# Sample attention's weighted sum of values: from three elementwise engines to 32-column products on TensorE

## The chip, the core and the metric

The kernel runs on one core of a Trainium2 chip. The metric is the device time of one launch in microseconds (us). Engines are named as the profile does: PE is TensorE, PEld its weight loads, DVE VectorE, ACT ScalarE, POOL GpSimd, SP the engine that issues every DMA here.

## The reference, cut to what matters

One decoder layer is computed for 1,024 prompt tokens and for eight sample tokens. Layer: an FFN, an input projection, two mixers (a gated recurrence and a differential attention, four heads each), an output projection, a second FFN. All of it is float32.

For a sample token the attention looks at 4,096 cached positions, 32 pages of 128, in each of four heads, with two softmax maps per head:

```python
p = jax.nn.softmax(jnp.concatenate(scores, axis=-1), axis=-1)
p = p.reshape(B, DA_HEADS, 2, Lq, p.shape[-1])
a = p[:, :, 0] - lam * p[:, :, 1]
...
    outs.append(jnp.einsum('bhqk,bkhv->bqhv', a[..., start:start + n], v.astype(jnp.float32)))
```

The last line is the one that the change concerns, for the cached part: eight rows, 32 pages, a page being 128 positions by four heads of 128 values, 256 KB.

## The kernel before

**Stages.** The prompt goes through the weights in two halves of 512 tokens; the eight sample tokens ride along as columns. `first_half` is FFN1 and the input projection, `second_half` the output projection and FFN2. The program's order is first half 0, first half 1, second half 0, second half 1. Weights come as tiles of 128x512 (`wr`), are split on ACT and DVE (partly POOL) into a high and a low part (`wH`, `wL`, seven buffers each), and every product is three PE passes (`mm3`, L376; L431 for the down projection; L498 for the input projection), in slices of 512, 264 or 256 columns. There are 672 such weight tiles; second half 1 begins with the 525th.

**Work beside.** `weave` interleaves two side streams with this main work, by credits: `mixer` (the prompt's recurrence and attention, one half at a time), and `sample_stream`: `sample_attention`, then `hgrn_sample`. Second half 1 needs the result of both for its second slice (the tile `oTs`). The framework then orders each engine's instructions by a simulated time line with priorities: main evacuations first, mixers next, the sample stream last. Engines run their instructions in that order, and SP's one DMA queue too.

**Sample attention.** For sample row b, `keys(b, i)` loads a page of keys, multiplies it on POOL (L954) and sums it on DVE (L955). When 32 pages are through, `softmax(b)` makes the weights `Sb` [128 positions, 32 pages, 8 maps]; its last instruction adds the two maps of a head (map two already carries minus lambda). `values(b, i)` then goes through 32 pages of values, one by one, interleaved with the keys of row b + 1: on even pages four DVE instructions, one a head, multiply by a weight and add to `sacc` [128, 512] (L1004); on odd pages four ACT instructions scale the page (L1006) and POOL adds it (L1008); page 0 is ACT's (L1002). `end(b)` sums `sacc` over the positions by four products with a column of ones (L1015).

**Rings that matter here.** Pages of both kinds, and the recurrence's states, share the ring `kv` of eight buffers in program order. PSUM tiles: `mm` (main work) three, `mx` two (until now the mixers alone), `my` two, and `nm` one: the sums of the norms, `softmax`, `end` and the recurrence take turns in it, in program order. So `norm_factors` of first half 1 (L270, L279), which comes after `end(2)` and `softmax(3)` in the program, cannot begin before these are through, and the evacuations of the input projection (L498) need its factors.

Of the kernel before, what the change touches and what calls it, by code (L numbers as in the profile page):

```python
# [18 lines left out]
P = 128  # L19
# [9 lines left out]
# columns of the constant table  # L29
C_ID, C_M, C_SUF, C_MSK, C_REL, C_SREL, C_SLP, C_QSC = 0, 128, 1152, 1280, 1728, 2752, 2784, 2792  # L30
C_N = 2800


def shape_constants():
# [5 lines left out]
    for l in range(7):  # L40
        s = 64 >> l
        mid = (t // (2 * s)) * 2 * s + s
        right = (t >= mid) & (j >= mid) & (j <= t)
        left = (t < mid) & (j > t) & (j < mid)
        c[:, C_M + (l + 1) * P:C_M + (l + 2) * P] = right | left
        same = (j // (2 * s)) == (t // (2 * s))
        # the columns of right halves alone
        c[:, C_MSK + l * 64:C_MSK + (l + 1) * 64] = (same & (j % (2 * s) < s))[:, (np.arange(P) // s) % 2 == 1]
# [6 lines left out]
    c[:, C_QSC:C_QSC + 8] = np.repeat(SLOPES, 2)[None, :] ** 2  # L55
    return c
# [3 lines left out]
def kernel(ctx: ExitStack, tc: tile.TileContext, I, O):  # L60
# [63 lines left out]
    slp = CT("slp", [P, 8])  # L124
    c1n = CT("c1n", [P, 512])
# [9 lines left out]
    def load_consts():  # L135
        SP.dma_start(srel, K[:, C_SREL:C_SREL + NPG])
        SP.dma_start(slp, K[:, C_SLP:C_SLP + 8])
        SP.dma_start(pages, I["page_table"].rearrange("b (o n) -> o (b n)", o=1))
        # lower bound: c1n = -(1 - lb) / 2 with lb the softmax over the two rows
# [13 lines left out]
        # lambda  # L153
# [11 lines left out]
        # gains of the mixers  # L165
# [18 lines left out]
    # rows of the sample tokens  # L184
# [15 lines left out]
    class Group:  # L200
        """tokens that pass the weights together: tiles as wide as the group"""
# [9 lines left out]
    class Slice:  # L211
        """columns of a group that one matrix product takes"""
# [53 lines left out]
    def norm_sums(sl):  # L266
        """sums of squares by block, down the partitions; the columns of each height"""
# [6 lines left out]
    def norm_spread(sl, R, r):  # L274
        """the factors along a row, on all partitions"""
# [23 lines left out]
    def scaled(gi, sl, d):  # L299
        """what norm_finish makes, but for the norm's factors: those come with the products' results"""  # L300
# [6 lines left out]
    def norm_row(sl):  # L307
        """the factors alone, along a row"""
# [26 lines left out]
    def xn_pair(w):  # L335
        """room for high and low parts: in one tile, or one each"""
# [13 lines left out]
    def wload(H, L, raw, src):  # L350
        # while DVE has the most to do, some of the low parts on Pool
# [7 lines left out]
    def wtile(src, c):  # L359
        """c columns of weights, from tiles of 512 / c blocks of rows: pairs of (high, low) parts"""  # L360
# [9 lines left out]
    def mm3(ps, W, sl):  # L370
        """ps = W^T x, weights stationary, in three passes"""
# [7 lines left out]
    FB = [2, 4, 4, 4, 4, 4]  # L379

    def ffn(pre, slices, done, deferred=False):
        wg, wu, wd = (I[pre + n] for n in ("_w_gate", "_w_up", "_w_down"))

        def gateup(f, hs):
# [30 lines left out]
            # by slices where what comes before goes by slices  # L415
# [104 lines left out]
    def evac(name, c, ps, tb, kind, row, factors):  # L520
        # of the norm: the factor, half of it, and the eps that it makes of EPS and of 64 EPS
# [15 lines left out]
        else:  # L537
# [9 lines left out]
            with tc.high_priority():  # L547
                if name == "aq":
                    # the scale of the scores over each head's slope comes with the norm
# [6 lines left out]
        # where it goes  # L556
# [15 lines left out]
        else:  # L572
# [3 lines left out]
            # high and low parts side by side, and so below each other once transposed  # L576
# [43 lines left out]
    def hgrn_head(b):  # L620
        """the logarithms of the decays"""
# [8 lines left out]
    def hgrn_block(b):  # L630
# [30 lines left out]
        def stage1(h, q):  # L661
            """decays of four levels (the first of the first half: the running one), and both sides' factors"""
# [19 lines left out]
        def stage2(h, q):  # L682
# [11 lines left out]
            def right(t, l):  # L694
                """the columns of right halves at a level"""
# [72 lines left out]
    def att_scores(h, b, KT):  # L768
        """softmax weights of both maps, combined"""
        negrel = hc["negrel"]  # L770
        n = (b + 1) * P
        # both parts of the queries, each against the keys' high and low parts
# [74 lines left out]
    def zcols(n):  # L847
        """rows of the sample tokens as columns, by heads"""
# [68 lines left out]
    def page(name, src, i):  # L917
        t = kv()
        if i % 4 == 0:
            # the next numbers are read only once earlier pages are on their way: few registers  # L920
# [6 lines left out]
    def sample_attention():  # L927
# [3 lines left out]
        # scores of the new keys  # L931
# [25 lines left out]
        def softmax(b):  # L957
# [32 lines left out]
            S4 = Sb.rearrange("p i (h j) -> p i h j", j=2)  # L990
            DVE.tensor_tensor(out=S4[:, :, :, 0], in0=S4[:, :, :, 0], in1=S4[:, :, :, 1], op=ALU.add)

        def values(b, i):
            a = S[b][0]
            vt = page("v", cv, b * NPG + i)
            if i == 0:
                S["acc"] = ST("sacc", [P, 512], bufs=1)
            acc = S["acc"]
            for h in range(4):
                hs, w = slice(h * P, (h + 1) * P), a[:, i, 2 * h:2 * h + 1]  # L1000
                if i == 0:
                    ACT.activation(acc[:, hs], vt[:, hs], AF.Copy, scale=w)  # L1002
                elif i in VDVE:
                    DVE.scalar_tensor_tensor(out=acc[:, hs], in0=vt[:, hs], scalar=w, in1=acc[:, hs], op0=ALU.mult, op1=ALU.add)  # L1004
                else:
                    ACT.activation(vt[:, hs], vt[:, hs], AF.Copy, scale=w)  # L1006
            if i and i not in VDVE:
# [252 lines left out]
```

## Time and profile before

| what | value |
|---|---|
| median of three runs | 2474.95 us (2472.2 to 2476.01) |
| span of the profiled execution | 2471.9 us |
| PE busy | 2304.7 us, 93% |
| DVE busy | 1827.5 us, 74% |
| ACT busy | 1071.8 us, 43% |
| POOL busy | 999.5 us, 40% |
| chain that ended last | PE 22% of the span, every other engine at most 1% |

The profiled execution's span lies 3.1 us below the median of the runs. Matmuls are pipelined: the duration of one is its latency, and the distance from start to start is what it costs when the next one waits behind it. PEclk is the share of full TensorE clock that was granted, as a mean of its two levels (1.2 and 2.4 GHz) over a stretch. The chain followed back from the end covers about the last quarter of the span.

### The profile page before, as it was taken

Reading aid. Unit: us, or ns where it says so; the run is one execution under the profiler, and the core shown is the slowest. Engines: PE = TensorE matmul, PEld = TensorE weight load, DVE = VectorE, ACT = ScalarE, POOL = GpSimd, SP = SyncE. Lnnn points to the kernel's source line nnn. Section 1 sums busy time; section 2 is a strip of 40 time slices with the busy share of each in tenths; the row PEclk is TensorE's granted clock in tenths of the full one; section 3 lists DMA queues with packets and bytes.
Section 4 is the critical chain, followed back from the end, with each engine's and each line's share of the span. In section 5 each row is a group of like instructions: output and inputs, shape, how many; then the busy total and the mean of one; then the engine's idle time right before and its main releaser. Section 6 shows DMA issues by size and latency. Waiting matters only on the chain. (4 is left out here: it accounts for less than half of the span.)

```text
span 2471.9 us, 44310 instructions
## 1 busy us (share of the span) xinstructions
PE 2304.7 (93%) x15101; PEld 2079.1 (84%) x15101; DVE 1827.5 (74%) x3750; ACT 1071.8 (43%) x2465; POOL 999.5 (40%) x788
## 2 busy tenths in 40 slices
PE   7999999989998978989899879889798999999999
PEld 6999999989877866767888767677687889999999
DVE  6555657596799796798798997997987766555554
ACT  4322324435544434545554643434465554322222
POOL 4100101381176374474684673785756310100000
PEclk9999999999998998999899999999999999999999
DMA  4332334684466467576785773566755652332332
GB/s 137 90 95 83 112 91 125 183 286 139 130 217 205 134 213 230 165 234 215 239 280 145 243 236 114 186 211 202 235 173 182 183 170 94 90 95 91 90 95 74
DMA packets 273396, 402.37 MB, mean 163 GB/s; under 512 B 29641, under 2 KB 104650, under 8 KB 273170
## 3 DMA queue, kind: packets, MB, share of 16 engines
q1 hardware_dynamic: 273170, 399.54, 52.0%
q8 instruction: 119, 1.95, 0.3%
q14 instruction: 107, 0.88, 0.1%
HBM read 361.22 MB, written 38.21 MB: 162 GB/s over the span
## 5 line engine op out<-in xcount | busy, mean ns | idle before, releaser
L376 PE MATMUL mm<-xn,wH 128*128 128x256 f32 (+2 forms) x4800 | 1121.8, 327 | 19.4 <-DVE xn L106 5.7
L376 PEld LDWEIGHTS mm<-xn,wH 128*128 128x128 f32 x4800 | 808.6, 192 | 94.8 <-DVE xn L106 8.1
L376 PE MATMUL mm<-xn,wL 128*128 128x256 f32 (+2 forms) x2400 | 782.7, 326 | 1.4 <-DVE wL L106 1.4
L106 ACT CAST wH<-wr 128x512 fp32r<-128x512 f32 x672 | 409.3, 617 | 518.1 <-PE mm L376 275.3
L106 DVE TENSOR_TENSOR wL<-wr,wH 128x512 fp32r<-128x512 f32 x504 | 414.7, 825 | 163.8 <-ACT wH L106 132.8
L431 PE MATMUL mm<-h,wH 128*128 128x264 f32 (+2 forms) x2112 | 487.0, 324 | 7.3 <-DVE ft L409 4.7
L376 PEld LDWEIGHTS mm<-xn,wL 128*128 128x128 f32 x2400 | 461.1, 192 | 36.8 <-DVE wL L106 1.8
L954 POOL TENSOR_TENSOR kv<-kv,ss 128x512 f32<-128x512 f32 x256 | 371.2, 1459 | 145.3 <-DMA kv<-in_cache_k 127.1
L431 PEld LDWEIGHTS mm<-h,wH 128*128 128x128 f32 x2112 | 349.9, 190 | 38.4 <-DVE ft L409 5.8
L411 POOL TENSOR_TENSOR ft<-ft,acc 128x256 f32<-128x256 f32 (+1 forms) x110 | 101.5, 922 | 656.6 <-DVE ft L409 645.9
L431 PE MATMUL mm<-h,wL 128*128 128x264 f32 (+2 forms) x1056 | 340.5, 323 | 0.0
L498 PE MATMUL mm<-wH,xn 128*128 128x256 f32 (+1 forms) x1728 | 325.5, 286 | 7.2 <-ACT ez L527 2.5
L106 POOL TENSOR_TENSOR wL<-wr,wH 128x512 fp32r<-128x512 f32 x168 | 237.9, 1417 | 223.0 <-ACT wH L106 184.7
L1004 DVE SCALAR_TENSOR_TENSOR sacc<-kv,sS,sacc 128x128 f32<-128x128 f32 x480 | 283.5, 645 | 20.4 <-POOL sacc L1008 20.4
L498 PEld LDWEIGHTS mm<-wH,xn 128*128 128x128 f32 (+1 forms) x1728 | 259.4, 180 | 17.5 <-ACT ez L527 3.2
L1006 ACT ACTIVATE kv<-kv,sS 128x128 f32<-128x128 f32 x512 | 164.5, 391 | 210.3 <-DMA kv<-in_cache_v 161.2
L498 PE MATMUL mm<-wL,xn 128*128 128x256 f32 (+1 forms) x864 | 246.2, 286 | 1.0 <-DVE wL L106 1.0
L1008 POOL TENSOR_TENSOR sacc<-sacc,kv 128x512 f32<-128x512 f32 x128 | 185.6, 1450 | 117.9 <-issue 27.3
L433 DVE SCALAR_TENSOR_TENSOR xr<-mm,xr 128x264 f32<-128x264 f32 (+2 forms) x288 | 146.0, 511 | 91.4 <-PE mm L431 91.0
L431 PEld LDWEIGHTS mm<-h,wL 128*128 128x128 f32 x1056 | 200.2, 190 | 14.7
L955 DVE TENSOR_REDUCE sS<-kv 128x8 f32<-128x512 f32 x256 | 170.8, 673 | 37.2 <-POOL kv L954 36.8
L498 PEld LDWEIGHTS mm<-wL,xn 128*128 128x128 f32 (+1 forms) x864 | 155.2, 180 | 4.7 <-DVE wL L106 1.2
(219 smaller groups left out, 2409.0 us busy)
## 6 DMA issues: line engine op xcount, KB each, us to landing
kv<-in_cache_k SPq DMA_DIRECT2D x256, 256.0 KB
kv<-in_cache_v SPq DMA_DIRECT2D x256, 256.0 KB
wr<-in_ffn_w_gate SPq DMA_DIRECT2D x176, 256.0 KB
wr<-in_ffn_w_up SPq DMA_DIRECT2D x176, 256.0 KB
wr<-in_ffn_w_down SPq DMA_DIRECT2D x176, 256.0 KB
wr<-in_w_in SPq DMA_DIRECT2D x96, 256.0 KB
aq<-qt SPq DMA_DIRECT2D x64, 128.0 KB
wr<-in_w_out SPq DMA_DIRECT2D x32, 256.0 KB
```

The source lines that it names most:

```text
L106: return ACT.copy(H, src), (eng or DVE).tensor_tensor(out=L, in0=src, in1=H.bitcast(F32), op=ALU.subtract)
L376: PE.matmul(ps[:, :w], a, b[k][:, :w], start=k == 0 and j == 0, stop=k == n - 1 and j == 2)
L411: POOL.tensor_tensor(out=t, in0=t, in1=sl.acc, op=ALU.mult)
L431: PE.matmul(ps[:, :w], a[:, cs], b[:, :w], start=j == 0 and q == 0, stop=j == m - 1 and q == 2)
L433: DVE.scalar_tensor_tensor(out=sl.xr[d][:, :w], in0=ps[:, :w], scalar=0.25, in1=sl.xr[d][:, :w], op0=ALU.mult, op1=ALU.add)
L498: PE.matmul(ps[:tb, 0:256], a, b, start=k == 0 and j == 0, stop=k == KC - 1 and j == 2)
L954: POOL.tensor_tensor(out=kt, in0=kt, in1=qb, op=ALU.mult)
L955: DVE.tensor_reduce(out=Sb[:, i], in_=kt.rearrange("p (n d) -> p n d", d=64), op=ALU.add, axis=AX.X)
L1004: DVE.scalar_tensor_tensor(out=acc[:, hs], in0=vt[:, hs], scalar=w, in1=acc[:, hs], op0=ALU.mult, op1=ALU.add)
L1006: ACT.activation(vt[:, hs], vt[:, hs], AF.Copy, scale=w)
L1008: POOL.tensor_tensor(out=acc, in0=acc, in1=vt, op=ALU.add)
```

## The change

The products of values and weights go to PE. Four pages are collected, then four float32 products follow, each with the 32 columns of weights of all four pages (4 pages x 8 maps) as stationary operand [128 x 32] and one page [128 x 512] as moving operand. Product j goes to the array's columns 32j to 32j+31 and to partitions 32j to 32j+31 of one `mx` tile. One DVE instruction adds that tile to `sacc` (or copies it, for the first group of a row). Of each product only the rows that belong to its page are wanted; `end(b)` selects them, sums the two maps and the four strips, by products with a constant matrix `vsel` in place of the ones. The last instruction of `softmax` falls away. Per launch: 480 DVE, 544 ACT and 128 POOL instructions go, 256 products (64 groups) and 64 DVE instructions come. The same 256 pages are loaded.

```diff
+    for r in range(P):
+        if r // 32 == r % 32 // 8:
+            c[r, C_SEL + r % 8 // 2] = 1.0
...
+    vsel = CT("vsel", [P, 4])
...
+        SP.dma_start(vsel, K[:, C_SEL:C_SEL + 4])
...
-            S4 = Sb.rearrange("p i (h j) -> p i h j", j=2)
-            DVE.tensor_tensor(out=S4[:, :, :, 0], in0=S4[:, :, :, 0], in1=S4[:, :, :, 1], op=ALU.add)
+        vts = {}

         def values(b, i):
-            a = S[b][0]
-            vt = page("v", cv, b * NPG + i)
-            if i == 0:
+            Sb = S[b][0]
+            vts[i % VP] = page("v", cv, b * NPG + i)
+            if i % VP < VP - 1:
+                return
+            if i == VP - 1:
                 S["acc"] = ST("sacc", [P, 512], bufs=1)
-            acc = S["acc"]
-            for h in range(4):
-                hs, w = slice(h * P, (h + 1) * P), a[:, i, 2 * h:2 * h + 1]
-                if i == 0:
-                    ACT.activation(acc[:, hs], vt[:, hs], AF.Copy, scale=w)
-                elif i in VDVE:
-                    DVE.scalar_tensor_tensor(out=acc[:, hs], in0=vt[:, hs], scalar=w, in1=acc[:, hs], op0=ALU.mult, op1=ALU.add)
-                else:
-                    ACT.activation(vt[:, hs], vt[:, hs], AF.Copy, scale=w)
-            if i and i not in VDVE:
-                POOL.tensor_tensor(out=acc, in0=acc, in1=vt, op=ALU.add)
-
-        VDVE = range(0, 32, 2)
+            po = MX()
+            w = Sb.rearrange("p i n -> p (i n)")[:, 8 * (i - VP + 1):8 * (i + 1)]
+            for j in range(VP):
+                PE.matmul(po[32 * j:32 * j + 32, :], w, vts[j], start=True, stop=True, tile_position=(0, 32 * j))
+            if i == VP - 1:
+                DVE.tensor_copy(S["acc"], po)
+            else:
+                DVE.tensor_tensor(out=S["acc"], in0=po, in1=S["acc"], op=ALU.add)
+
+        VP = 4

         def end(b):
             po = NM()
             for h in range(4):
-                PE.matmul(po[:, h:h + 1], S["acc"][:, h * P:(h + 1) * P], ones[:, 0:1], start=True, stop=True)
+                PE.matmul(po[:, h:h + 1], S["acc"][:, h * P:(h + 1) * P], vsel[:, h:h + 1], start=True, stop=True)
             DVE.tensor_copy(oT[:, :, b], po[:, 0:4])
```

Line numbers of the changed kernel are higher by 6 or 7 (L376 is L382, L431 L437, L498 L504, L270 L276); the products of values are L1011, `end` is L1022.

**Where PE's order changes.** In the changed program the 256 products of values stand on PE in 102 runs of neighbours: 45 single ones, 8 pairs, 16 triples, 26 fours, 4 fives, 2 eights and one seven. A single one stands between products of the main work, as here in the input projection of first half 1, after (buffer numbers kept; `mm` main work, `mx` the group's tile):

```order
L504 MATMUL mm_14752<-wH_14729,xn_13718 128x256
L1011 MATMUL mx_14722<-kv_14557,sS_12161 32x512
L504 MATMUL mm_14752<-wH_14729,xn_13719 128x256
L1011 MATMUL mx_14722<-kv_14624,sS_12161 32x512
L504 MATMUL mm_14752<-wL_14730,xn_13718 128x256
L1011 MATMUL mx_14722<-kv_14686,sS_12161 32x512
```

Here three of a group's four products each stand by themselves.

At the norm factors of first half 1, PE before, the softmax of sample row 3 (`sd`, `sn`) stands between products of the input projection (`mm`), and these go on up to the factors:

```order
L814 MATMUL my<-aV,aaT 128x128 x2
L970 MATMUL nm<-sd_14266,ones 128x8
L971 MATMUL nm<-sn,ident 128x8
L498 MATMUL mm<-wH,xn 128x256
L498 MATMUL mm<-wL,xn 128x256
```

After, the last main product ahead of this place stands in front of five groups of values, of which these rows are the end, then `end(2)`, the softmax and the factors (L276), with only the prompt's attention (L815, L820, L829) between them:

```order
L1011 MATMUL mx<-kv,sS 32x512 x2
L829 MATMUL my<-ident,aos 128x128
L815 MATMUL my<-ident,ap_13459 128x128 x4
L1022 MATMUL nm<-vsel,sacc 128x1 x4
L820 MATMUL my<-aV,aaT 128x128 x4
L971 MATMUL nm<-ident,sw 8x128
L976 MATMUL nm<-sd_13977,ones 128x8
L977 MATMUL nm<-sn,ident 128x8
L829 MATMUL my<-ident,aos 128x128
L987 MATMUL nm<-sw,ones 128x8
L276 MATMUL nm<-ones,acc 128x1 x4
L1011 MATMUL mx<-kv,sS 32x512 x8
```

The softmax and `end(2)` moved behind the main products that stood beside them before.

At the end of the sample stream, PE before, the recurrence's first steps (L853, `hgrn_sample`) stand among FFN2 of second half 0, with 31 weight tiles of it still to come:

```order
L376 MATMUL mm<-xn,wH 128x512
L786 MATMUL mx<-aKT,aq 128x512 x2
L786 MATMUL mx<-aKT,aq 128x256 x2
L853 MATMUL nm<-ident,kv 128x8
L823 MATMUL my<-ident,aos 128x128
L809 MATMUL my<-ident,ap_21071 128x128 x4
L853 MATMUL nm<-ident,kv 128x8 x3
L376 MATMUL mm<-xn,wH 128x512
```

After, all of second half 0 and the first product of second half 1 (slice of 256 columns) stand ahead of the last six groups (24 products) of row 7, of which these are the last two and a half; `end(7)` and the whole recurrence follow, then main work again:

```order
L820 MATMUL my<-aV,aaT 128x128 x8
L1011 MATMUL mx<-kv,sS 32x512 x5
L829 MATMUL my<-ident,aos 128x128
L1011 MATMUL mx<-kv,sS 32x512 x5
L1022 MATMUL nm<-vsel,sacc 128x1 x4
L859 MATMUL nm<-ident,kv 128x8 x4
L908 MATMUL nm<-s_22611,ones 128x32
L859 MATMUL nm<-ident,kv 128x8 x4
L889 MATMUL nm<-qTs,kv 128x1 x32
L859 MATMUL nm<-ident,kv 128x8 x4
L908 MATMUL nm<-s_22924,ones 128x32
L382 MATMUL mm<-xn,wH 128x264
```

The stream's end moved from inside second half 0 to the start of second half 1, with no main product beside it.

## Rows read from the trace of the kernel before

**Rows 1.** The page's part 1: busy time, share of the span, instructions.

```profile
PE 2304.7 (93%) x15101; PEld 2079.1 (84%) x15101; DVE 1827.5 (74%) x3750; ACT 1071.8 (43%) x2465; POOL 999.5 (40%) x788
```

**Rows 2.** Three stretches: PE, PEld, DVE, ACT, POOL busy, PEclk, DMA share, GB/s.

```profile
800.00:840.00 40.00, 40.00 (x208) 33.37 (x207) 27.77 (x70) 14.35 (x29) 8.04 (x7) 1.00 0.39 117
860.00:940.00 80.00, 63.33 (x272) 49.48 (x272) 78.74 (x138) 29.05 (x74) 62.92 (x46) 0.91 0.68 216
1395.00:1435.00 40.00, 33.14 (x212) 28.09 (x210) 39.54 (x73) 20.83 (x50) 31.26 (x21) 0.99 0.92 306
```

**Rows 3.** The same view: ahead of the values, and behind the sample attention.

```profile
0.00:494.00 494.00, 476.81 (x3919) 468.64 (x3920) 292.80 (x633) 180.75 (x381) 87.31 (x107) 1.00 0.38 114
494.00:675.00 181.00, 170.27 (x1307) 158.37 (x1306) 141.17 (x279) 84.57 (x172) 66.96 (x46) 0.97 0.59 187
1895.00:2472.00 577.00, 570.67 (x4345) 547.51 (x4344) 328.50 (x736) 215.64 (x452) 75.85 (x76) 0.99 0.36 109
```

**Rows 4.** The page's groups: busy us, mean ns | idle before; PE's main products.

```profile
L376 PE MATMUL mm<-xn,wH 128*128 128x256 f32 (+2 forms) x4800 | 1121.8, 327 | 19.4 <-DVE xn L106 5.7
L376 PE MATMUL mm<-xn,wL 128*128 128x256 f32 (+2 forms) x2400 | 782.7, 326 | 1.4 <-DVE wL L106 1.4
L431 PE MATMUL mm<-h,wH 128*128 128x264 f32 (+2 forms) x2112 | 487.0, 324 | 7.3 <-DVE ft L409 4.7
L498 PE MATMUL mm<-wH,xn 128*128 128x256 f32 (+1 forms) x1728 | 325.5, 286 | 7.2 <-ACT ez L527 2.5
```

**Rows 5.** Groups by form: one third of L376, and a DVE instruction that reads PSUM.

```profile
L376 PE MATMUL mm<-xn,wH 128*128 128x512 f32 x1600 | 536.0, 411 | 13.2 <-DVE xn L106 5.7 <-DVE xr L433 4.1 <-DVE xr L1052 1.6
L409 DVE TENSOR_TENSOR ft<-ft,mm 128x512 f32<-128x512 f32 x44 | 29.8, 678 | 11.9 <-PE mm L376 11.8
```

**Rows 6.** Chain that ended last: start us, length us, what; pieces of dense PE work.

```profile
1914.77 1.78 PE my L814 x16
...
1944.06 1.68 PE nm L883 x16
...
1964.59 5.11 PE mm L376 x22
...
2128.17 46.12 PE mm L376 x384
```

**Rows 7.** Instructions on the tile sacc: `end`, durations ns min/median/max.

```profile
L1015 PE MATMUL nm<-ones,sacc x64: 164/250/353, 816.5 to 1896.1; 128*128 128x1 f32 x64
```

**Rows 8.** The page's groups: the instructions on values that fall away.

```profile
L1004 DVE SCALAR_TENSOR_TENSOR sacc<-kv,sS,sacc 128x128 f32<-128x128 f32 x480 | 283.5, 645 | 20.4 <-POOL sacc L1008 20.4
L1006 ACT ACTIVATE kv<-kv,sS 128x128 f32<-128x128 f32 x512 | 164.5, 391 | 210.3 <-DMA kv<-in_cache_v 161.2
L1008 POOL TENSOR_TENSOR sacc<-sacc,kv 128x512 f32<-128x512 f32 x128 | 185.6, 1450 | 117.9 <-issue 27.3
```

**Rows 9.** Timeline of PE at the norm factors of first half 1.

```profile
1171.00 0.27 PE L965 MATMUL nm<-ident,sw 128*8 128x128 f32 x1
...
1181.59 0.29 PE L981 MATMUL nm<-sw,ones 128*128 128x8 f32 x2
...
1189.29 0.78 PE L498 MATMUL mm<-wH,xn 128*128 128x256 f32 x2
```

**Rows 10.** Timeline of SP: two page loads, one behind the other.

```profile
1209.20 0.34 SPq L924 DMA_DIRECT2D kv<-in_cache_v  x1
1209.78 0.34 SPq L924 DMA_DIRECT2D kv<-in_cache_k  x1
```

**Rows 11.** Chain that ended last, at the end of the sample stream.

```profile
1890.49 2.65 DMA kv<-zs_hv
...
1894.75 1.67 PE nm L1015 x8
...
1933.04 5.77 DMA kv<-zs_hv
```

More of the change, by code (lines that the diff above doesn't have):

```diff
@@ L27 @@
 SLOPES = [2.0 ** (-2.0 * (h + 1)) for h in range(4)]
-C_ID, C_M, C_SUF, C_MSK, C_REL, C_SREL, C_SLP, C_QSC = 0, 128, 1152, 1280, 1728, 2752, 2784, 2792
-C_N = 2800
+C_ID, C_M, C_SUF, C_MSK, C_REL, C_SREL, C_SLP, C_QSC, C_SEL = 0, 128, 1152, 1280, 1728, 2752, 2784, 2792, 2800
+C_N = 2804
 def shape_constants():
```

## The prediction

> **What bounds the kernel now.** I read the busy shares first. PE is busy 93% of the span, DVE 74% [rows 1]. That is an average over two kinds of stretch, which the view by stretches separates. Where the sample stream rests, as from 800 us, PE is busy 40 of 40 us at full clock and DVE has room [rows 2]. Where keys and values run, from 860 us, DVE is busy 78.7 of 80 us and PE only 63.3, at a granted clock of 0.91; likewise from 1395 us [rows 2]. So PE bounds the rests, and DVE the runs; a run loses a fifth to a quarter of what PE could do.
>
> How much is that in all? I add up what PE's instructions cost when they stand close. In the chain's dense pieces 22 products of 512 columns take 5.11 us, 0.232 us each, and 384 of 264 and 256 columns take 46.12 us, 0.120 us each [rows 6]. L376 has 7,200 products, a third of them with 512 columns [rows 4, 5]: 2,400 x 0.232 + 4,800 x 0.120 = 1,133 us. L431 has 2,112 and half as many low parts, also in thirds [rows 4]: 498 us. L498 has 1,728 and half as many low parts at 0.120: 311 us. The other 2,141 of the 15,101, mostly float32 with 128 columns or fewer at 0.11 us [rows 6], come at 0.12 to 257 us. Sum: 2,199 us. Of the span of 2,471.9 us, 273 us are then not used by PE. Outside the middle (up to 675 us, from 1895 us) PE sat idle for 17, 11 and 6 us and lost some 11 us by the clock [rows 3]; with latencies that nothing follows I put 60 us there. The middle loses 213 us. That is all that relief of DVE could give back.
>
> **The change part by part.** *Removed:* 283.5 us on DVE, 164.5 on ACT, 185.6 on POOL [rows 8]. *Added on DVE:* 64 instructions of 128x512 that read PSUM, at 0.68 us by L409 [rows 5], 44 us. DVE is 240 us freer, all of it in runs, so DVE no longer bounds them. The load of `vsel`, and the addition that `softmax` loses, I cost at nothing: one small DMA ahead of the middle, eight DVE instructions in a DVE that has room.
>
> *Added on PE:* 256 float32 products with 512 columns. A float32 product is two passes: `end` has 32 products and 64 instructions [rows 7]. No row shows a float32 pass of 512 columns. It can't be faster than 0.232 us, what a pass of the other type takes [rows 6]. 128 columns take 1.78 / 16 = 0.111 us [rows 6], so 512 take at most 0.444; but one column takes 1.68 / 16 = 0.105 [rows 6], so there the weight load may be what one sees. I take 0.43, near the upper end, since L814 is the row with the same operand type. What the strips give has no row at all. Three cases for the 102 runs on PE:
> - nothing overlaps: 512 x 0.43 = 220 us;
> - a strip's second pass overlaps the next strip's first, but the two passes of one product follow one another and PE starts in order: a run of n costs n + 1 passes, (256 + 102) x 0.43 = 154 us;
> - the strips of a group run fully side by side: 109 pairs of passes, 94 us.
>
> I take 154, the case that needs only what PE's order allows. With passes at 0.232 us it is 83 us, and fully side by side 51; these are the lower bounds.
>
> A rule of the Trainium skill speaks against the change: TensorEngine Tiling (Array Packing), Key Properties, says that a change of tiling mode drains the engine. No run of before has strips, so no row shows it. By it each of the 204 changes of mode would cost at most what a product's latency exceeds its spacing, 0.411 - 0.232 us [rows 5, 6], some 37 us in all, and the sum below would be 2,587.
>
> *Moved: the sample stream's place.* It has the lowest priority, and its values now wait for PE, the busiest engine. In PE's order it lags: `end(1)`, `end(5)` and `end(6)` stand 28 to 46 weight tiles later than before. It must catch up at two places, and there PE stands before its own next product with nothing else in the queue.
>
> At the norm factors of first half 1, five groups, `end(2)` and `softmax(3)` stand behind the last main product. The pages of a group can be loaded only when the group before has left its buffers (four of the eight). So a group costs seven page loads at 0.58 us [rows 10], a landing, and five passes: 4 + 3 (the chain has 2.65 to 5.77 [rows 11]) + 2 = 9 us. Four such distances are 36 us; softmax takes 10.6 us from its first product to its last, and 7.7 more pass until the main products resume [rows 9]. Of these 54 us PE fills about 17 (five groups and the prompt's attention): 37 lost, where before about 6 were. If the pages lie ready, 10; if each load is slow, 55.
>
> At the end of the stream six groups and the recurrence stand alone. Without keys, two groups are in the ring; 1 MB a group at the best rate seen, 306 GB/s [rows 2], is 3.4 us, and issue, landing and passes, two groups at a time, give about 4: 24 us. From `end(7)` to the last product of the recurrence before took from 1894.75 to 1945.7 us, 51 us [rows 6, 11], beside other work; on free engines I take 40. Less 17 us that PE fills, and 3 for restarting, 50 lost; 30 to 70.
>
> Behind SP's waits for these buffers stand weight loads; eleven tiles (four raw, seven split) of twelve products, 31 us at 0.232, cover them. For the rest of the middle, where groups meet late pages and stages start, I leave 50 us (30 to 80).
>
> *Sum.* 2,199 + 60 + 154 + 37 + 50 + 50 = 2,550 us of span, against 2,471.9; the median of the runs lies 3.1 above the span, which is within the rounding. Its own range, from the bounds of the waits and some of the passes' price: 2,490 to 2,610.
>
> **The rivals.** *Faster: the strips overlap and the waits are short.* For it: PE's fours stand together, every engine but PE has room, and runs now lose a fifth to a quarter of PE. Price: 94 us for the products, waits of 15 and 25, rest 30: 2,199 + 60 + 164 = 2,423. It decides against mine once products and waits together stay below the 213 us that the middle loses today.
> The skill's TensorE: Matmul & The Clock Gate, Measured speedup vs the span model, gives 2.38 times for three products on three column strips. By that the products would cost about 105 us; no run here has shown it.
>
> *Slower still: strips don't overlap, and modes drain.* For it: nearly half of the runs are single products between main ones. 220 + 37 + 137 for the waits: 2,653.
>
> *Pages become the bound.* Values can't be loaded ahead of their group, and SP holds weight loads behind them. If the cover of 31 us is used up, each of 64 groups costs 2 us of PE, 128 in place of 50: 2,628.
>
> *No change.* What DVE gives back, PE takes: 213 us for the four terms, 2,472.
>
> **How the numbers follow.** Mine 0.41, the faster case 0.25, strips that don't overlap 0.20, pages 0.08, no change 0.06. A measurement of this kernel tells about 0.2% (5 us) from nothing. Faster 0.25, same 0.06, slower 0.69. The range must reach into both neighbours: 2,425 (half of the faster case is left out) to 2,650 (half of the slowest).
>
> **What would show it.** Right: DVE busy falls by more than 200 us; in the middle PE is near 100% in runs too, with DVE near 65%; two holes in PE, one of some 40 us ahead of L276 and one of 40 to 60 us between the last main product of second half 0 and the first of slice two; neighbours of L1011 on different strips start 0.43 us apart, not 0.01 and not 0.86. Wrong: the four first passes of a group starting together, holes of under 20 us, or runs with DVE still at 95%.

## The result, and the profile after

The changed kernel takes 2,509.8 us (median of four, 2,504.9 to 2,519.8), beside 2,474.1 us for the kernel before on the same chip: ratio 1.0152, 95% interval 1.0129 to 1.0174. It is slower, by 36 us where 76 were forecast. The profiled execution has a span of 2,509.2 us, 37.3 more than before.

Busy time by engine, from the page (us, share of the span, instructions), to be held against [rows 1]:

```profile
PE 2403.2 (96%) x15613; PEld 2078.4 (83%) x15613; DVE 1585.9 (63%) x3326; ACT 924.8 (37%) x1921; POOL 788.2 (31%) x660
```

DVE fell by 242 us, PE rose by 98. The stretches of [rows 2] and [rows 3], and the two places where the forecast saw holes (PE, PEld, DVE, ACT, POOL busy, PEclk, DMA share, GB/s):

```profile
860.00:940.00 80.00, 79.94 (x396) 62.10 (x395) 60.37 (x132) 24.43 (x49) 33.22 (x25) 1.00 0.56 169
1395.00:1435.00 40.00, 37.70 (x261) 33.77 (x260) 29.04 (x60) 16.36 (x32) 16.00 (x12) 1.00 0.76 245
1120.00:1240.00 120.00, 93.63 (x555) 71.23 (x554) 84.33 (x164) 46.50 (x120) 60.82 (x51) 0.83 0.81 258
2000.00:2080.00 80.00, 59.05 (x312) 42.15 (x313) 34.91 (x112) 27.92 (x73) 11.94 (x4) 0.74 0.68 209
```

The first two rows are the relief: PE busy 79.94 of 80 us where it had 63.33 [rows 2], with DVE at 60.37. The last two are what it costs: PE idles 26 of 120 us and 21 of 80 us, and a lower clock comes with it. The kernel before, in the same two stretches:

```profile
1120.00:1240.00 120.00, 110.11 (x676) 98.55 (x676) 93.01 (x194) 68.40 (x180) 64.75 (x52) 0.94 0.72 229
2000.00:2080.00 80.00, 78.37 (x580) 73.45 (x579) 51.56 (x132) 43.00 (x97) 3.42 (x5) 1.00 0.46 141
```

The new work itself, from the groups by line (busy us, mean ns | idle before):

```profile
L1011 PE MATMUL mx<-kv,sS 128*32 128x512 f32 x512 | 127.7, 652 | 7.8 <-DMA kv<-in_cache_v 4.7 <-DVE sS L995 2.6 <-DVE atn L794 0.5
L1015 DVE TENSOR_TENSOR sacc<-mx,sacc 128x512 f32<-128x512 f32 x56 | 38.4, 685 | 37.9 <-PE mx L1011 37.8
L1013 DVE COPY sacc<-mx 128x512 f32<-128x512 f32 x8 | 5.5, 688 | 11.4 <-PE mx L1011 11.4
```

**How the strips run.** PE's timeline (start us, length us, what) around the first products of the trace, and at one whole group:

```profile
665.94 1.04 PE L1011 MATMUL mx<-kv,sS 128*32 128x512 f32 x2
666.91 0.50 PE L650 MATMUL mx<-hgL,sufr 128*128 128x512 f32 x1
667.25 0.40 PE L651 MATMUL mx<-hgH,sufr 128*128 128x512 f32 x1
667.58 1.06 PE L1011 MATMUL mx<-kv,sS 128*32 128x512 f32 x6
668.57 0.50 PE L382 MATMUL mm<-xn,wL 128*128 128x512 f32 x1
668.90 0.39 PE L382 MATMUL mm<-xn,wH 128*128 128x512 f32 x1
...
680.40 1.07 PE L1011 MATMUL mx<-kv,sS 128*32 128x512 f32 x8
681.40 0.50 PE L382 MATMUL mm<-xn,wH 128*128 128x512 f32 x1
```

One product (x2, two passes) holds PE for 0.97 us, from 665.94 to 666.91; three hold it for 0.99 and four for 1.00. Inside the group of four the records of the four first passes start 7 ns apart, the four second passes 434 ns after the last of them and again 7 ns apart, and the next main product 522 ns after that. The strips run side by side, and a run costs the same whether one, three or four of them are filled. PE's order has 102 runs (rows of products with nothing between); with each last pass at its 0.52 us they cost 122 us. At the lengths of full clock, with no wait inside, they would cost 106; the other 15 us stand in nine runs, at the low clock or with a wait for a page in their middle.

The neighbours pay too. The main product ahead of a run is followed after 0.327 us in place of 0.233, and the one behind it after 0.336 (668.57 to 668.90 above): some 0.2 us a run, 20 us for 102, which the account below puts with the stretches in which the runs stand.

**Where the time went.** I price all other work of PE as the prediction did (2,199 us in both kernels) and take from each stretch what its work costs; the rest is time that PE lost to waits, latency and a low clock. Worked out from every PE record of the two traces, in us:

| | products | 1100 to 1260 | 1960 to 2120 | rest of 580 to 1960 | outside | sum with 2,199 |
|---|---|---|---|---|---|---|
| before | 0 | 26 | 5 | 194 | 50 | 2,474 |
| after | 122 | 40 | 36 | 55 | 57 | 2,509 |

(The sums agree with the spans to 2 us. How the small products are priced decides the split between the last two columns: with the prediction's flat 0.12 us for each, "rest" reads 198 and 64, "outside" 44 and 50. The other columns move by 1 us.) Relief of DVE gave back 139 us of the 194 that the middle lost. The products took 122 of it, the two holes 45, and the stretches outside 7 more.

### The profile page after: what moved, and what is told of

Same layout as the page of the kernel before. It is cut to its first block, busy times and chain, and to the rows that moved or that the text cites. A ratio compares the mean times of both kernels' runs of the same rounds, so it can differ in the third digit from the quotient of the medians.

```text
span 2509.2 us, 44115 instructions
## 1 busy us (share of the span) xinstructions
PE 2403.2 (96%) x15613; PEld 2078.4 (83%) x15613; DVE 1585.9 (63%) x3326; ACT 924.8 (37%) x1921; POOL 788.2 (31%) x660
## 4 chain that ended last, share of the span: by engine, by line
PE 62%; DVE 6%; DMA 6%; POOL 2%; issue 1%; ACT 1%; SPq 0%; POOLq 0%; DVEq 0%; ACTq 0%
PE mm L382 33%; PE mm L437 12%; PE mm L504 6%; PE mx L1011 4%; DMA kv<-in_cache_k 3%; PE my L705 1%; POOL kv L960 1%; PE mx L792 1%; PE my L820 1%; DVE sS L961 1%; DVE wL L110 1%; DMA kv<-in_cache_v 1%; PE my L815 0%; DVE hXR L678 0%; DMA kv<-zs_hv 0%
## 5 line engine op out<-in xcount | busy, mean ns | idle before, releaser
L382 PE MATMUL mm<-xn,wH 128*128 128x256 f32 (+2 forms) x4800 | 1107.8, 324 | 16.0 <-ACT xn L110 6.8
L382 PEld LDWEIGHTS mm<-xn,wH 128*128 128x128 f32 x4800 | 799.2, 190 | 102.6 <-issue 20.1
L382 PE MATMUL mm<-xn,wL 128*128 128x256 f32 (+2 forms) x2400 | 775.7, 323 | 0.0
L960 POOL TENSOR_TENSOR kv<-kv,ss 128x512 f32<-128x512 f32 x256 | 353.9, 1388 | 443.6 <-DMA kv<-in_cache_k 339.2
L382 PEld LDWEIGHTS mm<-xn,wL 128*128 128x128 f32 x2400 | 455.8, 190 | 42.6 <-issue 9.2
L437 PE MATMUL mm<-h,wH 128*128 128x264 f32 (+2 forms) x2112 | 482.1, 321 | 0.7 <-DVE xr L439 0.3
L437 PEld LDWEIGHTS mm<-h,wH 128*128 128x128 f32 x2112 | 347.7, 188 | 36.6 <-issue 5.0
L437 PE MATMUL mm<-h,wL 128*128 128x264 f32 (+2 forms) x1056 | 339.3, 321 | 0.0
L504 PE MATMUL mm<-wH,xn 128*128 128x256 f32 (+1 forms) x1728 | 322.0, 286 | 5.4 <-DVE ft L478 2.6
L110 POOL TENSOR_TENSOR wL<-wr,wH 128x512 fp32r<-128x512 f32 x168 | 228.6, 1362 | 284.5 <-ACT wH L110 235.7
L504 PEld LDWEIGHTS mm<-wH,xn 128*128 128x128 f32 (+1 forms) x1728 | 257.4, 180 | 24.5 <-issue 11.2
L504 PE MATMUL mm<-wL,xn 128*128 128x256 f32 (+1 forms) x864 | 245.9, 285 | 3.3 <-POOL wL L110 3.3
L437 PEld LDWEIGHTS mm<-h,wL 128*128 128x128 f32 x1056 | 198.7, 188 | 18.1 <-issue 3.4
L504 PEld LDWEIGHTS mm<-wL,xn 128*128 128x128 f32 (+1 forms) x864 | 154.8, 179 | 8.8 <-POOL wL L110 3.5
L1011 PE MATMUL mx<-kv,sS 128*32 128x512 f32 x512 | 127.7, 652 | 7.8 <-DMA kv<-in_cache_v 4.7
L415 DVE TENSOR_TENSOR ft<-ft,mm 128x256 f32<-128x256 f32 (+2 forms) x132 | 67.0, 508 | 73.5 <-PE mm L382 73.3
L110 ACT CAST h<-ft 128x256 fp32r<-128x256 f32 (+2 forms) x132 | 63.1, 478 | 97.7 <-POOL ft L417 75.3
```

The source lines that it names most:

```text
L110: return ACT.copy(H, src), (eng or DVE).tensor_tensor(out=L, in0=src, in1=H.bitcast(F32), op=ALU.subtract)
L382: PE.matmul(ps[:, :w], a, b[k][:, :w], start=k == 0 and j == 0, stop=k == n - 1 and j == 2)
L415: DVE.tensor_tensor(out=t, in0=t, in1=pu[:, :sl.w], op=ALU.mult)
L437: PE.matmul(ps[:, :w], a[:, cs], b[:, :w], start=j == 0 and q == 0, stop=j == m - 1 and q == 2)
L504: PE.matmul(ps[:tb, 0:256], a, b, start=k == 0 and j == 0, stop=k == KC - 1 and j == 2)
L960: POOL.tensor_tensor(out=kt, in0=kt, in1=qb, op=ALU.mult)
```

## Experiments

Line numbers move by one to three where an edit adds lines. Each run was compared with the kernel before on its own chip (2,471 to 2,474 us).

**The four products of a group on one strip**

```diff
-                PE.matmul(po[32 * j:32 * j + 32, :], w, vts[j], start=True, stop=True, tile_position=(0, 32 * j))
+                PE.matmul(po[0:8, :], w[:, 8 * j:8 * j + 8], vts[j], start=j == 0, stop=j == VP - 1)
...
```

The additions on DVE and the products of `end` then take eight rows in place of 128, and the stationary operand has 8 columns in place of 32. A lone product still holds PE for 0.96 us (0.97 in the changed kernel).

> The four products of a group go to the same eight rows of the sum, one behind the other, in place of four strips (the result is the same sum). Theory 'the strips run side by side and a group costs about as much as a lone product': 256 products x 2 passes x 0.43 us = 220 us of TensorE in place of some 125 us, so 2,595 to 2,615 us, and the passes of L1011 no longer start a few ns apart. Rival 'what costs time is the waits around the products, the strips are worth little': 2,500 to 2,530 us.

Measured: 2,625.9 us, 1.0616 (1.0592 to 1.0640). PE's timeline at one group:

```profile
838.02 0.39 PE L382 MATMUL mm<-xn,wH 128*128 128x512 f32 x1
838.34 3.60 PE L1011 MATMUL mx<-kv,sS 128*8 128x512 f32 x8
841.87 0.88 PE L705 MATMUL my<-hXR,hE 128*128 128x64 f32 x6
```

The products in the groups by line:

```profile
L1011 PE MATMUL mx<-kv,sS 128*8 128x512 f32 x512 | 243.2, 602 | 3.4 <-DMA kv<-in_cache_v 2.0 <-DVE atn L794 1.4
```

A group now holds PE for 3.53 us in place of 1.00, and L1011 is busy 243.2 us in place of 127.7. These 116 us are as much as the whole difference between the two kernels: what PE loses elsewhere adds up to 192 us for 188, though it lies in other places (the two holes lose 35 us less, the rest 40 more). Strips are worth what their overlap saves; the median is some 10 us above the range expected. The passes stand 0.43 us apart, the price that the prediction took.

**The group computed twice**

```diff
-            for j in range(VP):
-                PE.matmul(po[32 * j:32 * j + 32, :], w, vts[j], start=True, stop=True, tile_position=(0, 32 * j))
+            for r in range(2):
+                for j in range(VP):
+                    PE.matmul(po[32 * j:32 * j + 32, :], w, vts[j], start=True, stop=True, tile_position=(0, 32 * j))
```

> Each group of four products is computed twice into the same bank (the second pass overwrites the first). Theory 'the products are worth their passes on TensorE, those of one group together': two passes more for each of 64 groups, 0.87 us, so 56 us more if the four stay together and 89 us more if each of the 102 runs has its own: 2,565 to 2,600 us. Rival 'the cost of a group is the change between products and main work, not its passes': under 2,535 us.

Measured: 2,577.7 us, 1.0427 (1.0405 to 1.0450): 68 us more, between the 56 and 89 of the two cases. The products are busy 204.8 us in place of 127.7. So 68 of these 77 us go into the time: the products are worth their passes on PE, nearly one for one.

**No products**

```diff
-                PE.matmul(po[32 * j:32 * j + 32, :], w, vts[j], start=True, stop=True, tile_position=(0, 32 * j))
...
-                DVE.tensor_tensor(out=S["acc"], in0=po, in1=S["acc"], op=ALU.add)
+                DVE.tensor_tensor(out=S["acc"][:, j:j + 1], in0=vts[j][:, 0:1], in1=w[:, j:j + 1], op=ALU.mult)
```

> Left out: the value products and the additions of their sums, so the cached values' share of the sample attention; the pages are loaded as before and each is read by one operation of one column on VectorE. Theory 'the products cost their own time on TensorE, 64 groups in some 102 runs of 1.2 us': 2,380 to 2,400 us, the holes stay. Rival 'they also make the rest wait (changes of the array's layout, banks, VectorE's additions)': under 2,350 us.

Measured: 2,358.0 us, 0.9543 (0.9524 to 0.9563), between the two expectations: 152 us under the changed kernel, 157 by the spans, of which passes are 122. The other 35 are waits that go with the products, which the theory wanted to stay: by the account at the end of this section the two holes lose 60 us less, the rest of the middle 32 more and the stretches outside 8 less (the 20 us that the runs' neighbours pay are among these sums). Three stretches of the kernel without products: the first hole; the second, by the same times; and the second by the same place in the program, which comes earlier here:

```profile
1100.00:1260.00 160.00, 150.75 (x1057) 140.75 (x1056) 116.17 (x232) 74.73 (x148) 83.54 (x63) 0.97 0.77 256
2000.00:2080.00 80.00, 80.00 (x669) 80.00 (x669) 44.23 (x88) 22.85 (x44) 5.96 (x8) 1.00 0.31 92
1873.00:1962.00 89.00, 85.26 (x591) 78.03 (x590) 55.20 (x116) 39.44 (x86) 5.13 (x5) 1.00 0.50 150
```

Between the same main products as in the changed kernel's 1,960 to 2,120 us, PE loses some 5 us here. The last multiplication of keys (L960) is over by 1,669 us, in the changed kernel by 1,943: once values no longer stand in PE's order, the stream runs ahead of the main work.

**The products ahead in the scheduler's order**

```diff
-            for j in range(VP):
-                PE.matmul(po[32 * j:32 * j + 32, :], w, vts[j], start=True, stop=True, tile_position=(0, 32 * j))
+            with hp(3000):
+                for j in range(VP):
+                    PE.matmul(po[32 * j:32 * j + 32, :], w, vts[j], start=True, stop=True, tile_position=(0, 32 * j))
...
+                    DVE.tensor_tensor(out=S["acc"], in0=po, in1=S["acc"], op=ALU.add)
```

> The value products and the addition behind them are put ahead of the other work in the scheduler's order; the work is the same. Theory 'the two holes of TensorE, at the norm factors of the first half and at the end of the sample stream, are left because the stream comes last on TensorE': the stream ends earlier, some of the 75 us of the holes goes, 2,435 to 2,495 us. Rival 'the pages set the stream's pace': TensorE then waits at the products for pages, 2,505 to 2,560 us, and the wait of L1011 on a DMA grows.

Measured: 2,492.3 us, 1.0075 (1.0053 to 1.0096), 17 us less and at the upper end of what was expected. The reason given holds in small part. The traced execution took 2,504.3 us, 12 above the median; it has the hole at the end nearly as it was:

```profile
2000.00:2080.00 80.00, 60.21 (x347) 46.87 (x346) 33.87 (x108) 28.48 (x75) 11.95 (x4) 0.77 0.68 205
```

By the account at the end the two holes lose 10 us less there, the rest of the middle 18 more. What went besides is runs of products: 90 in place of 102, for 106 us in place of 122. With this priority 41 of them have four products, where 26 had. Where the other 12 us of the median's gain come from, no trace shows.

**The norm factors in the ring of the main products**

```diff
-            R, parts = norm_sums(sl)
+            R, parts = norm_sums(sl, MM())
...
-        R = NM()
+        R = MM()
         norm_spread(sl, R, sl.r[:, 0])
```

> The norm factors of the halves take their PSUM bank from the ring of the main products in place of the small ring that the sample stream shares. Theory 'the hole between 1,120 and 1,240 us is a wait for the small ring behind the stream': that hole of some 39 us goes, 2,470 to 2,490 us. Rival 'the hole is the dependence on the last columns of the half before, whatever the bank': 2,505 to 2,515 us.

Measured: 2,500.5 us, 1.0117 (1.0100 to 1.0134): 9 us less, between the two. In the changed kernel PE's timeline reads (in brackets the idle time ahead, and its releaser):

```profile
1187.00 0.59 PE L976 MATMUL nm<-sd,ones 8*128 8x8 f32 x2 [3.17 <-DVE sd L975]
...
1192.33 0.56 PE L987 MATMUL nm<-sw,ones 128*128 128x8 f32 x2 [3.91 <-DVE sw L985]
1193.22 1.87 PE L276 MATMUL nm<-ones,acc 128*128 128x1 f32 x8 [0.33 <-DVE sw L988]
```

L276 stands behind the stream's softmax (L976, L987) in the same ring. With its own bank it comes 51 us earlier:

```profile
1142.55 1.87 PE L276 MATMUL mm<-ones,acc 128*128 128x1 f32 x8 [3.58 <-DVE acc L260]
```

So the ring was that wait's cause. Between 1,100 and 1,260 us PE now loses 26 us in place of 40, but between 1,260 and 1,440 it loses 29 in place of 16. The stream, still behind, meets PE later. What stays of the gain lies in the products, 114 us for 122, and at the end, 31 us for 36.

**A larger share of the interleaving for the stream**

```diff
-    S0, S1, S2 = 0.4, 0.65, 0.85
+    S0, S1, S2 = 0.5, 0.8, 1.05
```

> The sample stream gets a larger share of the interleaving (0.5, 0.8, 1.05 in place of 0.4, 0.65, 0.85); the work is the same. Theory 'the hole at the end of the sample stream is there because it ends too late': the stream ends before 1,950 us, the hole between 2,000 and 2,080 us goes, 2,465 to 2,490 us. Rival 'what the stream gains at its end TensorE loses at the pages, which come faster than VectorE and the loads allow': 2,500 to 2,540 us.

Measured: 2,478.5 us, 1.0025 (1.0011 to 1.0040): 31 us less, in the theory's range. The stream does end earlier: the last product of `end` is at 1,873 us (2,038 in the changed kernel) and that of the recurrence at 1,932 us (2,063), so both lie beside main products. But the hole that the theory named is only halved, and more of the gain comes at the norm factors. The two holes:

```profile
1120.00:1240.00 120.00, 117.02 (x699) 89.53 (x698) 85.53 (x170) 54.59 (x133) 64.46 (x52) 1.00 0.82 266
2000.00:2080.00 80.00, 70.09 (x504) 65.09 (x503) 42.89 (x119) 39.69 (x91) 2.84 (x6) 0.96 0.36 107
```

By the account at the end PE loses 11 us at the norm factors in place of 40 and 17 at the end in place of 36, and 11 more in the rest of the middle; the products still cost 126 us. So three numbers take back 31 of the 36 us by which the change is slower. The kernel before was not run with this share, so how much of the 31 us it would gain too is open.

**The three edits together**, with the diffs of the last three.

> Three edits together: the products ahead in the scheduler's order, the norm factors in the ring of the main products, and the larger share of the stream. If the holes are separate causes, each edit keeps what it gives: 18 and 9 us measured apart, and some 30 us for the share, 2,440 to 2,465 us, faster than before the change. If they are one slack that moves about: 2,480 to 2,500 us.

Measured: 2,483.4 us, 1.0044 (1.0029 to 1.0059), no better than the share alone. The gains don't add. Bringing the stream forward and giving the norm factors a bank of their own shorten the same wait, and the gain in runs of products is gone: there are 117 here, with the share alone 122, with the priority alone 90.

**Eleven buffers of pages**

```diff
-    NKV = 8
+    NKV = 11
```

> The ring of pages has 11 buffers in place of 8, nothing else. Rival 'pages are the bound, since a group of four keeps half of the ring': the pages are loaded earlier, 2,470 to 2,495 us. Theory 'TensorE is the bound, the pages wait for the products in TensorE's order': 2,500 to 2,512 us.

Measured: 2,507.2 us, 1.0135 (1.0113 to 1.0158), within the noise of the changed kernel. With this order of PE the ring of pages is not the bound. POOL's wait for pages of keys, the longest on the list of waits that names pages, is 339.2 us in the changed kernel and 322.8 here, and the time stays. The larger ring was not run together with the whole groups that follow.

**Groups issued whole**

```diff
-            for j in range(VP):
-                PE.matmul(po[32 * j:32 * j + 32, :], w, vts[j], start=True, stop=True, tile_position=(0, 32 * j))
+            last = None
+            for j in reversed(range(VP)):
+                with tc.issue_after(last.ins) if last is not None else nullcontext(), hp(9000 if last is not None else 0):
+                    last = PE.matmul(po[32 * j:32 * j + 32, :], w, vts[j], start=True, stop=True, tile_position=(0, 32 * j))
```

> The product on the page that is loaded last is issued first, and the three others of its group right behind it on TensorE, with nothing between; the work is the same. TensorE's order then has 62 runs of products (60 of four, 2 of eight) where the changed kernel has 102. Theory 'a run costs its two passes however many strips it fills': 60 x 0.97 + 2 x 1.84 = 62 us in place of 128, so some 65 us less, 2,440 to 2,465 us. Rival 'the cost goes by the products, or the group waits longer for its last page': 2,495 to 2,520 us.

Measured: 2,517.6 us, 1.0171 (1.0144 to 1.0198). The saving is there and the time isn't: by the account the products fell from 122 to 72 us (64 would be 62 runs at full clock), and PE lost it elsewhere. The traced execution took 2,528.5 us, 11 above the median. The products in the groups by line:

```profile
L1013 PE MATMUL mx<-kv,sS 128*32 128x512 f32 x512 | 75.6, 667 | 25.7 <-DMA kv<-in_cache_v 21.6 <-DVE atn L794 2.8 <-ACT hE L674 1.2
```

PE's timeline at the end of the first half:

```profile
1183.49 1.94 PE L1013 MATMUL mx<-kv,sS 128*32 128x512 f32 x8 [4.00 <-DMA kv<-in_cache_v]
1185.36 1.65 PE L820 MATMUL my<-aV,aaT 128*128 128x128 f32 x6
1188.85 0.45 PE L829 MATMUL my<-ident,aos 128*128 128x128 f32 x1 [1.84 <-DVE aos L827]
1189.09 1.06 PE L815 MATMUL my<-ident,ap 128*128 128x128 f32 x4
1192.24 1.94 PE L1013 MATMUL mx<-kv,sS 128*32 128x512 f32 x8 [2.09 <-DMA kv<-in_cache_v]
```

A whole group stops PE until its fourth page has landed (4.00 us, 2.09 us), and the prompt's attention (L820, L815) stands behind it. Direct waits for pages of values rose from 4.7 to 21.6 us. The clock fell with the pauses; the same group takes 1.94 us here and 1.07 at 680.40 in the changed kernel. The stretch by engine, clock 0.74 where the changed kernel has 0.83:

```profile
1120.00:1240.00 120.00, 86.84 (x474) 64.84 (x473) 83.06 (x176) 46.88 (x121) 63.49 (x53) 0.74 0.80 259
```

By the account each hole loses 12 us more than in the changed kernel and the rest of the middle 43 more; the parts of these 43 I haven't traced. The edit also gives three products of each group a high priority, and no run separates that from the grouping.

**Whole groups and the larger share**, the diffs of both.

> Groups issued whole, as in the run before, and the larger share of the stream (0.5, 0.8, 1.05). If the two are separate, 65 and 31 us: 2,405 to 2,435 us, faster than before the change. If the share only moved the same slack: within 15 us of the run with whole groups alone.

Measured: 2,455.9 us, 0.9926 (0.9898 to 0.9953), some 20 us above the range expected, but 54 under the changed kernel and 0.7% faster than before the change. The products:

```profile
L1013 PE MATMUL mx<-kv,sS 128*32 128x512 f32 x512 | 67.8, 604 | 12.4 <-DMA kv<-in_cache_v 4.7 <-ACT hE L674 3.6 <-DVE atn L794 3.0
```

With a stream that is ahead, a whole group finds its pages: 4.7 us of waits for them in place of 21.6. Saving on runs and share of the stream are worth something together that whole groups alone are not. In time the grouping is worth 23 us here (2,478.5 to 2,455.9), though the products cost 63 us less. Much of the rest stands in the middle, where DVE is near its limit once more, busy 72.0 of 80 us where the changed kernel has 58.5:

```profile
1290.00:1370.00 80.00, 66.28 (x486) 57.24 (x484) 72.01 (x133) 28.40 (x67) 58.90 (x47) 0.94 0.86 271
```

**A still larger share (0.6, 0.9, 1.2), with whole groups**

> Groups issued whole and a still larger share of the stream (0.6, 0.9, 1.2). Theory 'the hole at the stream's end goes when the recurrence ends before the main products of the second half need the lanes': 2,400 to 2,425 us. Rival 'the stream packed tighter meets VectorE, which then sets the pace in the middle as it did before the change': 2,425 to 2,460 us.

Measured: 2,479.2 us, 1.0031 (1.0016 to 1.0045). Neither range: slower than both expected, on the rival's side. PE loses 42 us between 1,260 and 1,440 us and 39 between 1,100 and 1,260, against 33 and 19 with the smaller share. The rival's cause isn't shown: between 1,260 and 1,440 us DVE is busy 140.9 us here and 142.1 with the smaller share, while PE's direct waits for pages of values rose from 4.7 to 11.8 us in all. The theory falls too. The last product of the recurrence is at 1,757 us, 170 earlier than with the smaller share, and the hole near 2,000 us is still there:

```profile
2000.00:2080.00 80.00, 69.52 (x505) 65.04 (x503) 43.22 (x123) 40.28 (x95) 2.70 (x5) 0.94 0.34 102
```

Between 1,960 and 2,120 us PE loses 20 us with the stream long over, where the changed kernel loses 36. It waits there for the prompt's attention (L792, L815, L820, L829: 7.3 us) and for a split of the main work (3.2 us). So not all of that hole belongs to the stream's end.

**Whole groups, the share 0.5, 0.8, 1.05, and the norm factors' own ring**

> Groups issued whole, the larger share of the stream (0.5, 0.8, 1.05), and the norm factors in the ring of the main products; the kernel with the first two took 2,456 us. Theory 'the wait for the small ring at the norm factors is worth its 9 us wherever the stream stands': 2,440 to 2,452 us. Rival 'with a stream that ends earlier and groups that come whole, the wait at that place is for other things': 2,452 to 2,470 us.

Measured: 2,462.7 us, 0.9966 (0.9952 to 0.9980). The rival's case: with a stream that ends earlier and whole groups, the edit brings nothing (7 us more, at the edge of the noise); PE loses 18 us between 1,100 and 1,260 where it lost 19.

The same account as above for the runs on which the verdicts rest, in us of PE:

| | runs | products | 1100 to 1260 | 1960 to 2120 | rest of 580 to 1960 | outside |
|---|---|---|---|---|---|---|
| after | 102 | 122 | 40 | 36 | 55 | 57 |
| no products | 0 | 0 | 15 | 1 | 87 | 49 |
| products ahead | 90 | 106 | 33 | 33 | 73 | 59 |
| larger share | 122 | 126 | 11 | 17 | 66 | 57 |
| whole groups | 62 | 72 | 52 | 48 | 98 | 58 |
| whole, larger share | 62 | 63 | 19 | 27 | 88 | 57 |

## Why the prediction was right or wrong, point by point

- **What bounds the kernel: right.** DVE bounded the stretches with keys and values, 194 us of PE were lost there, and 139 came back when DVE was relieved. DVE fell by 242 us (forecast: over 200); in the two stretches shown PE is busy 100% and 94%, DVE 75% and 73% (forecast: near 65%).
- **The direction: right, and its mechanism:** what DVE gives back, PE takes for the products and for waits at two places where the late stream stands alone.
- **The products' term: mis-sized, and this is the step that failed.** It said 154 us, by n + 1 passes for a run of n neighbours; it measured 122. The assumption "a strip's second pass overlaps the next strip's first, but the two passes of one product follow one another and PE starts in order" is false. All first passes of a run start together, then all second passes, which the prediction had named as the sign that would prove it wrong. For a run of four it priced 2.15 us, and 1.00 was measured; the case put down as a lower value, "fully side by side", 94 us, was the right mechanism. It lacked 12 us for the edges of the runs and the 7 ns between strips, and 15 us for the nine runs at low clock or with a wait inside. A single product was priced too low, at 0.86 us where it holds PE for 0.97 and its neighbours for 0.2 more. The price of a pass, 0.43 us, was right.
- **The change of tiling mode.** Into a run of products the last main product is followed after 0.327 us in place of 0.233 (median of 33 and of 2,210 pairs on L382), the last pass is followed after 0.522 in place of 0.430, and the first main product behind after 0.336 in place of 0.233 (24 pairs). That is 0.29 us for each of 102 runs, 30 us, a third of which is in the 122. The Trainium skill's rule (TensorEngine Tiling (Array Packing), Key Properties, that a change of mode drains the engine) agrees with a cost at either edge, and the bound of 37 us that the prediction worked out beside it holds. But the kernel with all products on one strip shows the same 0.33, 0.52 and 0.34 us, so several strips are not what it goes by; eight-column products may be of the same mode, and no run separates that.
- **The addition on DVE: right,** 43.9 us for 44.
- **The hole at the norm factors: right in size, by luck in part.** It is 40 us between 1,100 and 1,260 for 37, but 26 of it were lost in that stretch before, where the prediction had 6 at that place. Its cause was right in part: the wait for the softmax's ring is real and can be taken away, but that gives 9 us and no more.
- **The hole at the end: right in place, too large by 14 us,** 36 for 50. `end(7)` and the recurrence took 26 us on free engines, from 2,037 to 2,063, in place of the 40 put. The 51 us of before from which the 40 were taken stop short: L883 is not the recurrence's last line, its last product is L902 at 1,954, 59 us after 1,894.75. And the cause is right in part only: with the stream over at 1,757 us, 20 us are still lost there.
- **The rest of the middle, 55 for 50, and outside it, 57 for 60:** 112 for 110 as a sum, whichever way it is split (114 by the flat price). The 50 was a guess, and these stretches also hold most of the 20 us that the runs' neighbours pay, which the prediction's sum didn't have; so that it fits is luck in part. Together: 154 to 122 is 32 us, the end 14, against 3 and 5 the other way and 3 outside: 2,550 less 41 is the span of 2,509.
- **The rivals.** The faster case had the strips right and the waits wrong: 15, 25 and 30 us were put where 40, 36 and 55 stand, 61 us; those alone make its 2,423 a 2,484, and its price of 94 in place of 122 the rest. Strips that don't overlap were measured by themselves: 2,626, near the 2,653 put. Pages as the bound fall with the ring of eleven buffers, and by PE's direct waits for pages of values, 4.7 us in all; they come back as 21.6 us once groups are issued whole. The Trainium skill's 2.38 times for three products on three column strips (TensorE: Matmul & The Clock Gate, Measured speedup vs the span model) was nearer than my own assumption: the prediction's estimate by it was 105 us, and 122 were measured. Here four products take 1.00 us on four strips and 3.53 on one, 3.5 times.
- **What I had not weighed** is that the number of runs, not of products, is the price. 45 of 102 runs are a single product at nearly the price of four. An order that keeps groups whole saves PE 50 to 63 us of products; in time it gave nothing alone (8 us more) and 23 us with a stream that is early enough for the pages.

## What to carry to other kernels

When work moves to the engine that bounds the kernel, price it by the stops it makes in that engine's order: here a stop costs 1.0 us with one strip or with four, and 0.2 more in the products beside it, so what shares a stop should be issued together. Moved work also takes over that engine's queue discipline. A stream of lowest priority that now needs the busiest engine falls behind and must catch up alone at the stage ends; give it a larger share of the interleaving first (31 us here, for three numbers; with whole groups a still larger one lost 23 us again), and only then take away single waits: of the 14 us that the norm factors' own bank saved while the stream was late, 13 came back at the next stage.

## What the hardware showed that I had not expected

- Two-pass float32 products on four column strips are interleaved by passes: four first passes 7 ns apart, four second passes 434 ns later. The group holds PE for 1.00 us, a lone product for 0.97.
- A run of narrow float32 products costs some 0.29 us at its edges (0.327 for 0.233 us ahead, 0.522 for 0.430 at its last pass, 0.336 for 0.233 in the main product behind), with four strips and with one alike. Full-width float32 products cost next to nothing there: 0.232 us ahead of L705 (median of 20), and behind it the main product takes 0.317 us but starts 0.084 after the last pass.
- Here a pause of a few us is paid for twice. In the stretch from 1,120 to 1,240 us the granted clock is 0.83 in the changed kernel and 0.74 with whole groups. With whole groups it is 0.54 from 1,180 to 1,195 us, nearly all of it at the lower of the two levels, 1.2 GHz; the groups of four there take 1.94 us, and 1.07 where 1.00 is granted (2.4 GHz). What PE did before, from 1,159 to 1,183 us, is stand nine times for 0.2 to 4.0 us, for the attention's operands and for a page.
